# Six start offsets for the activations of the down products in a float32 decoder layer

## The chip, the cores and the metric

The kernel runs on one core of one Trainium2 chip. The metric is the device time of one execution in microseconds. The profile is of one execution of its own.

## The reference, cut to what matters

One decoder layer in float32, for 256 tokens of 2048 features. It has a feed-forward part at each end; between them stand a mixer (windowed attention beside a recurrent part) and a cross-attention, which the change does not touch. Each feed-forward part is

```
def swiglu(h, w_gate, w_up, w_down):
    return (jax.nn.silu(h @ w_gate) * (h @ w_up)) @ w_down

x = x + 0.5 * swiglu(rms_norm(x, ffn1_norm[l]), ffn1_w_gate[l], ffn1_w_up[l], ffn1_w_down[l])
```

with 5632 features inside (w_gate and w_up are 2048 x 5632, w_down is 5632 x 2048). The second feed-forward part is the same with its own weights, and a norm follows it.

## The kernel before

**Products.** All large products are made from pairs of float32r parts. A weight tile arrives as float32 (raw or raw2, by DMAs of SP's queue, `load`); ACT copies it into a float32r part `hi` (L299) and DVE subtracts to get the rest `lo` (L300), in `divide`. The activations are split in the same way into a hi and a lo part: xhi and xlo for the normed input, hhi and hlo for what goes into the down product. For each chunk of 128 features TensorE (PE) then runs three matmuls into the same bank of PSUM (`multiply`): activation hi by weight hi (L336), activation hi by weight lo (L337), activation lo by weight hi (L338). The activations are the stationary operand, 128 features by 128 tokens, loaded anew for each matmul; the weights are the moving one, as a rule 512 columns. `product` makes 512 output columns for all 256 tokens: it takes a unit of two chunks of weights at a time, and runs them for both halves of the tokens. So a unit is 12 matmuls.

**A feed-forward part.** `feed_forward` works in three groups (GROUPS) of four, four and three blocks of 512 inner features. For each block j it makes the gate product, applies silu on ACT (L415) into hb, makes the up product, and multiplies on DVE (L418). The block is then transposed in the background, by `transposed`: PE transposes 128 x 128 pieces of hb into PSUM (L347), two chunks at a time, ACT copies them to hhi (L352), and DVE subtracts to get hlo (L353). When the blocks of the group are through, four down products (n = 0 to 3) take all of the group's chunks, 16 or 12, out of hhi and hlo, and DVE adds half of the result to x (L427). So a group has 4 x 2 x 3 x 16 = 384 down matmuls, or 288 in the group of three blocks; the two feed-forward parts have 2112 in six groups.

**Tiles.** hhi and hlo are taken once per group, each from one buffer of the pool of its feed-forward part (bufs=1), as [128, 16, 256] float32r: 16 KB in each partition. A chunk is 256 tokens, 1024 bytes, and a matmul's stationary operand is half of it, 512 bytes. `Act.at` gives the slice. Each pool first takes a tile of 64 bytes (`aligned`) and so shifts all that follows. In the built program x, xhi, xlo, hhi, hlo, hb, raw, raw2, hi and lo, and the split activations of the mixer and the cross-attention, all start 480 bytes past a multiple of 512. In a weight tile of 288 columns, which is used once, the second half starts 1152 bytes after the first. Constants (the identity of the transposes among them) and the mixer's small tiles start elsewhere.

**Order.** Each engine runs its instructions in the order in which the Python code issues them. Background work (`Interleave`) is issued step by step between matmuls. Weight loads are issued some units ahead, and the hi and lo parts two units ahead.

Of the kernel before, what the change touches and what calls it, by code (L numbers as in the profile page):

```python
# [8 lines left out]
F32R = mybir.dt.float32r  # L9
# [6 lines left out]
P = 128  # L16
T = 256
# [103 lines left out]
def decoder_layer(ctx: ExitStack, tc: tile.TileContext, a: dict, out: bass.AP):  # L121
# [190 lines left out]
    def product(x: Act, w, skew=False):  # L312

        pw, _, nk, _, n = plan[at["product"]]
        assert pw.tensor is w.tensor
        at["product"] += 1
        o = [acc() for _ in range(2)]
        skewed = range(nk - AHEAD * KU - KU, nk, KU) if skew else range(nk, nk)
        for k in range(0, nk - KU * len(skewed), KU):
            bg.until(lambda: all(k + i in x.done for i in range(KU)))  # L320
            u = next_unit()
            for t in range(2):
                multiply(o[t][:, :n], x, u, k, t, nk)
                bg.tick()
        last = [(k, next_unit()) for k in skewed]
        for t in range(2):
            for k, u in last:
                multiply(o[t][:, :n], x, u, k, t, nk)
        return o
# [10 lines left out]
    def feat(tok, cols):  # L340


        b = tr()
        for i, col in enumerate(cols):
            for t in range(2):
                o = (2 * i + t) * P
                pe.transpose(b[:, o : o + P], tok[:, t, col : col + P], ident[:])  # L347
        return b[:].rearrange("p (c t) -> p c t", c=2)

    def split(x: Act, c, n, src):  # L350

        act.copy(x.at(0, c, n), src)  # L352
        dve.tensor_tensor(x.at(1, c, n), src, f32(x.at(0, c, n)), ALU.subtract)  # L353
        x.done |= set(range(c, c + n))
# [41 lines left out]
        return [r[:, t : t + 1] for t in range(n)]  # L396


    def feed_forward(sp, x, norm: Norm, wg, wu, wd, done, last=False):
        for gi, (j0, nj) in enumerate(GROUPS):  # L400
            h = Act(
                [sp.tile([P, 16, T], F32R, tag="hhi", name="hhi")],
                [sp.tile([P, 16, T], F32R, tag="hlo", name="hlo")], 16,
            )

            def transposed(hb, c):
                for q in range(2):
                    split(h, c + 2 * q, 2, feat(hb, [2 * q * P, (2 * q + 1) * P]))
                    yield

            for j in range(j0, j0 + nj):
                pg = product(norm.x, wg)
                hb = sp.tile([P, 2, 512], F32, tag="hb", name="hb", bufs=3)
                for t in range(2):
                    act.activation(hb[:, t, :], pg[t][:], AF.Silu, scale=norm.r[t])  # L415
                pu = product(norm.x, wu)
                for t in range(2):
                    dve.scalar_tensor_tensor(  # L418
                        hb[:, t, :], pu[t][:], norm.r[t], hb[:, t, :], ALU.mult, ALU.mult
                    )  # L420
                bg.spawn("feat", transposed(hb, 4 * (j - j0)))
            for n in range(4):
                end = gi == len(GROUPS) - 1
                pd = product(h, wd, skew=last and end and n == 3)
                for t in range(2):
                    xs = x[:, t, n * 512 : (n + 1) * 512]
                    dve.scalar_tensor_tensor(xs, pd[t][:], 0.5, xs, ALU.mult, ALU.add)  # L427
                if end:
                    done(n)
# [17 lines left out]
    with tc.tile_pool(name="f1", bufs=1, reuse_waits="tile") as sp:  # L447
        aligned(sp)
        at["pool"] = sp
        x = sp.tile([P, 2, D], F32, name="x")  # L450

        def col(n):
            return x[:, :, n * 512 : (n + 1) * 512]

        n1 = Norm(g_ffn1)
        for c in (slice(0, 256), slice(256, 512)):
            nc.sync.dma_start(x[:, :, c], W["x"][:, c].rearrange("(t p) n -> p t n", p=P))
            load(c.start // 256)
        for n in range(1, 4):
            nc.sync.dma_start(col(n), blk(W["x"], n))  # L460
            load(n + 1)
        for n in range(4):
            bg.spawn("feat", n1.block(n, col(n)))
        bg.spawn("const", late_vectors())
        hold = {}

        def done1(n):
            if n == 0:
                hold["n"] = Norm(g_mix)
            pool.dma_start(blk(x1d, n), col(n))  # L470
            bg.spawn("feat", hold["n"].block(n, col(n)))

        feed_forward(sp, x, n1, W["ffn1_w_gate"], W["ffn1_w_up"], W["ffn1_w_down"], done1)
        n2 = hold["n"]
        bg.drain()
        at["pool"] = None
# [666 lines left out]
    with tc.tile_pool(name="f2", bufs=1, reuse_waits="tile") as sp:  # L1143
# [18 lines left out]
        def done2(n):  # L1162
            for t in range(2):
                xs = x[:, t, n * 512 : (n + 1) * 512]
                act.activation(junk_t[:], xs, AF.Square, accum_out=ss[:, t, n : n + 1])  # L1165
                if n < 3:
                    pool.tensor_tensor(xs, xs, fin[:, n * 512 : (n + 1) * 512], ALU.mult)  # L1167

        feed_forward(
            sp, x, n4, W["ffn2_w_gate"], W["ffn2_w_up"], W["ffn2_w_down"], done2, last=True  # L1170
        )
# [42 lines left out]
```

## Time and profile before

| what | value |
|---|---|
| device time, median of 3 runs | 2328.53 us (2326.44 to 2334.17) |
| the profiled execution | 2327.99 us |
| its span, first to last instruction | 2326.3 us |
| mean granted TensorE clock | 0.998 |
| PE matmul records with xhi or xlo, 512 or 288 columns | 6048 |
| PE matmul records with hhi or hlo, 512 columns | 2112 |
| DVE L300, one of 128 x 1024 | 1226 ns mean, x769 |
| ACT L299, one of 128 x 1024 | 1048 ns mean, x769 |
| DMA, mean over the span | 186 GB/s |

How to read it. The page gives for each engine its busy time and its share of the span. PE counts matmul records, PEld the weight loads beside them. Matmuls overlap, and a record is longer than the distance to the next one; the distance is read from the starts in a timeline. Section 4 of the page follows the chain of work that ended last back to the start. In a group's line the last number is the idle time of its engine just before it, with what ended it. A windows view gives, for each stretch, its length, each engine's busy time with the number of instructions, the granted clock, and the share and rate of DMA.

The stretches of the six down groups in the span are 192.2 to 280.0 us, 457.2 to 544.9 and 677.6 to 746.5 in the first feed-forward part, and 1765.7 to 1853.4, 2030.6 to 2118.4 and 2251.1 to 2317.4 in the second.

### The profile page before, as it was taken

The page shows a single profiled execution, that of the slowest core. Times are in us where ns is not written, and L with a number is a line of the kernel's source. Part 1 is how long each engine was busy: PE and PEld are TensorE (multiplying, and loading weights), DVE is VectorE, ACT ScalarE, POOL GpSimd, SP SyncE. Part 2 cuts the span into 40 slices and gives each one's busy share as a digit, 9 for nine tenths or more (in the row PEclk, how much of TensorE's full clock was granted, in tenths as well). Part 3 has the DMA queues.
Part 4 walks back from the last instruction along what each step waited for, and adds up shares of the span by engine and source line. Part 5 has one row for each costly group of instructions (what it writes and reads, how often), then busy time and mean ns, then how long its engine had stood idle before and what let it go on. Part 6 is the DMA issues. An engine that isn't in the chain of part 4 may idle for free.

```text
span 2326.3 us, 27347 instructions
## 1 busy us (share of the span) xinstructions
PE 2303.9 (99%) x10853; PEld 1895.5 (81%) x10853; DVE 1259.5 (54%) x1395; ACT 1078.2 (46%) x1425; POOL 130.3 (6%) x192
## 2 busy tenths in 40 slices
PE   8999999999999999999999999999999999999998
PEld 7888888888888877888888878888888888888887
DVE  4545544554556477795444556555545544554545
ACT  5444344434445477444344446455444344434444
POOL 1000000000000000201220030001000000000001
PEclk9999999999999999999999999999999999999999
DMA  8555655556554544676432576648555555555553
GB/s 291 181 196 184 198 186 194 184 196 194 186 189 152 173 129 145 197 230 206 123 103 88 174 246 217 199 156 297 195 184 194 189 196 184 196 185 195 193 187 127
DMA packets 219856, 432.71 MB, mean 186 GB/s; under 512 B 14267, under 2 KB 17040, under 8 KB 219728
## 3 DMA queue, kind: packets, MB, share of 16 engines
q1 hardware_dynamic: 211520, 405.58, 53.3%
q0 software_dynamic: 8176, 25.38, 3.4%
q8 instruction: 85, 1.39, 0.2%
q14 instruction: 43, 0.35, 0.0%
q10 hardware_dynamic: 32, 0.01, 0.0%
HBM read 417.56 MB, written 13.11 MB: 185 GB/s over the span
## 4 chain that ended last, share of the span: by engine, by line
PE 93%; issue 4%; DVE 1%; DMA 1%; ACT 1%; POOL 1%; SPq 0%; POOLq 0%; ACTq 0%
PE acc L336 28%; PE acc L338 28%; PE acc L337 28%; PE tr L347 2%; PE mm L924 1%; PE tr L893 1%; POOL ml L1046 0%; PE mm L542 0%; DMA raw<-in_ffn_w_gate_dram 0%; PE tr L911 0%; ACT hi L299 0%; PE tr L994 0%; PE tr L907 0%; PE tr L581 0%; PE tr L589 0%
## 5 line engine op out<-in xcount | busy, mean ns | idle before, releaser
L300 DVE TENSOR_TENSOR lo<-raw,hi 128x1024 fp32r<-128x1024 f32 (+1 forms) x769 | 942.1, 1226 | 956.3 <-ACT hi L299 955.6
L299 ACT CAST hi<-raw 128x1024 fp32r<-128x1024 f32 (+1 forms) x769 | 805.5, 1048 | 1066.1 <-PE acc L338 1028.8
L336 PE MATMUL acc<-hi,xhi 128*128 128x512 f32 (+1 forms) x2016 | 798.7, 396 | 0.4 <-ACT xhi L373 0.4
L337 PE MATMUL acc<-lo,xhi 128*128 128x512 f32 (+1 forms) x2016 | 785.4, 390 | 0.0
L338 PE MATMUL acc<-hi,xlo 128*128 128x512 f32 (+1 forms) x2016 | 784.6, 389 | 0.0
L336 PEld LDWEIGHTS acc<-hi,xhi 128*128 128x128 f32 x2016 | 379.7, 188 | 80.3 <-issue 3.4
L338 PEld LDWEIGHTS acc<-hi,xlo 128*128 128x128 f32 x2016 | 379.1, 188 | 79.5 <-issue 1.0
L337 PEld LDWEIGHTS acc<-lo,xhi 128*128 128x128 f32 x2016 | 379.9, 188 | 78.0 <-issue 3.6
L336 PE MATMUL acc<-hi,hhi 128*128 128x512 f32 x704 | 275.5, 391 | 0.0
L338 PE MATMUL acc<-hi,hlo 128*128 128x512 f32 x704 | 274.2, 389 | 0.0
L337 PE MATMUL acc<-lo,hhi 128*128 128x512 f32 x704 | 274.0, 389 | 0.0
L338 PEld LDWEIGHTS acc<-hi,hlo 128*128 128x128 f32 x704 | 132.1, 188 | 27.5
L337 PEld LDWEIGHTS acc<-lo,hhi 128*128 128x128 f32 x704 | 132.2, 188 | 27.2
L336 PEld LDWEIGHTS acc<-hi,hhi 128*128 128x128 f32 x704 | 132.2, 188 | 26.8
L336 PE MATMUL acc<-hi,mthi 128*128 128x512 f32 x128 | 51.2, 400 | 0.0
L338 PE MATMUL acc<-hi,mtlo 128*128 128x512 f32 x128 | 50.1, 392 | 0.0
L337 PE MATMUL acc<-lo,mthi 128*128 128x512 f32 x128 | 49.9, 390 | 0.0
L1167 POOL TENSOR_TENSOR x<-x,fin 128x512 f32<-128x512 f32 x6 | 8.9, 1505 | 695.4 <-ACT junk L1165 695.4
L470 POOL DMA_DIRECT2D x1d<-x x4 | 3.0, 744 | 710.4 <-DVE x L427 710.4
L415 ACT ACTIVATE hb<-acc,rs 128x512 f32<-128x512 f32 x44 | 30.2, 690 | 19.5 <-PE acc L338 19.5
L352 ACT CAST hhi<-tr 128x512 fp32r<-128x512 f32 x44 | 25.7, 583 | 16.3 <-PE tr L347 16.3
L373 ACT ACTIVATE xhi<-tr,gains 128x256 fp32r<-128x256 f32 x48 | 22.0, 470 | 21.8 <-DVE xlo L374 16.1
(289 smaller groups left out, 1632.7 us busy)
## 6 DMA issues: line engine op xcount, KB each, us to landing
raw<-in_ffn_w_up_dram SPq DMA_DIRECT2D x88, 1024.0 KB, 5.1
raw<-in_ffn_w_down_dram SPq DMA_DIRECT2D x88, 1024.0 KB, 5.0
raw<-in_ffn_w_gate_dram SPq DMA_DIRECT2D x86, 1024.0 KB, 5.1
raw<-in_w_in_dram SPq DMA_DIRECT2D x136, 512.0 KB, 3.5
raw<-in_w_out_dram SPq DMA_DIRECT2D x32, 512.0 KB, 4.6
raw<-in_w_proj_attn_dram SPq DMA_DIRECT2D x16, 512.0 KB, 3.8
raw<-in_w_proj_rwkv_dram SPq DMA_DIRECT2D x16, 512.0 KB, 5.5
raw<-in_w_cross_kv_dram SPq DMA_DIRECT2D x16, 512.0 KB, 3.6
```

The source lines that it names most:

```text
L299: act.copy(hi[:, s], raw[:, s])
L300: dve.tensor_tensor(lo[:, s], raw[:, s], f32(hi[:, s]), ALU.subtract)
L336: pe.matmul(o, xh, hi[:, i, :], start=k + i == 0, stop=False)
L337: pe.matmul(o, xh, lo[:, i, :], start=False, stop=False)
L338: pe.matmul(o, xl, hi[:, i, :], start=False, stop=k + i == nk - 1)
L347: pe.transpose(b[:, o : o + P], tok[:, t, col : col + P], ident[:])
L352: act.copy(x.at(0, c, n), src)
L373: last = act.activation(self.x.at(0, c), b[:, j, :], AF.Copy, scale=g)
L415: act.activation(hb[:, t, :], pg[t][:], AF.Silu, scale=norm.r[t])
L893: pe.matmul(b[e][:, m * P : (m + 1) * P], x1[r, j, cs_], x2[r, j, cs_], start=True, stop=True,)
L924: pe.matmul(vb[:, o : o + P][:, r], lhs(e), rhs[:, r], start=first and e == 0, stop=True, **ek,)
L1167: pool.tensor_tensor(xs, xs, fin[:, n * 512 : (n + 1) * 512], ALU.mult)
```

## The change

Each of the six groups takes hhi and hlo out of a longer tile, of 16 x 256 + 64 elements (256 bytes more), and starts in it at another element: 8 times 1, 2, 4, 5, 6 and 7, that is 32, 64, 128, 160, 192 and 224 bytes. Both parts of a group have the same offset in their tile. The list is used up in the order of the groups, three in the first feed-forward part and three in the second.

```diff
+    places = [1, 2, 4, 5, 6, 7]
+
     def feed_forward(sp, x, norm: Norm, wg, wu, wd, done, last=False):
         for gi, (j0, nj) in enumerate(GROUPS):
-            h = Act(
-                [sp.tile([P, 16, T], F32R, tag="hhi", name="hhi")],
-                [sp.tile([P, 16, T], F32R, tag="hlo", name="hlo")], 16,
-            )
+            o = 8 * places.pop(0)
+
+            def part(name):
+                p = sp.tile([P, 16 * T + 64], F32R, tag=name, name=name)
+                return p[:, o : o + 16 * T].rearrange("p (c t) -> p c t", c=16)
+
+            h = Act([part("hhi")], [part("hlo")], 16)
```

Since the hhi tile is 256 bytes longer, the hlo tile begins 256 bytes later than before, and what lies behind both (hb, and raw2 in the second part) 512 bytes later.

## The prediction

> **What bounds the kernel now.** I read the page first: the busy times, the chain that ended last, then the groups of the down products.
>
> ```profile
> span 2326.3 us, 27347 instructions
> PE 2303.9 (99%) x10853; PEld 1895.5 (81%) x10853; DVE 1259.5 (54%) x1395; ACT 1078.2 (46%) x1425; POOL 130.3 (6%) x192
> ...
> PE 93%; issue 4%; DVE 1%; DMA 1%; ACT 1%; POOL 1%; SPq 0%; POOLq 0%; ACTq 0%
> ...
> L336 PE MATMUL acc<-hi,hhi 128*128 128x512 f32 x704 | 275.5, 391 | 0.0
> L338 PE MATMUL acc<-hi,hlo 128*128 128x512 f32 x704 | 274.2, 389 | 0.0
> L337 PE MATMUL acc<-lo,hhi 128*128 128x512 f32 x704 | 274.0, 389 | 0.0
> ```
>
> PE is busy for 99% of the span and carries 93% of the chain. The down products are 3 x 704 = 2112 matmuls, and nothing made them wait (idle 0.0). So PE's stream is the bound, and what counts in it is the distance from one matmul's start to the next, the pitch. The 389 ns of a record is no pitch: records overlap. The timeline of PE, early in the first down group, gives the pitch:
>
> ```profile
> 195.62 0.60 PE L347 MATMUL tr<-ident,hb 128*128 128x128 f32 x4
> 195.98 0.48 PE L336 MATMUL acc<-hi,hhi 128*128 128x512 f32 x1
> 196.30 0.40 PE L337 MATMUL acc<-lo,hhi 128*128 128x512 f32 x1
> 196.53 0.40 PE L338 MATMUL acc<-hi,hlo 128*128 128x512 f32 x1
> ...
> 197.92 0.39 PE L338 MATMUL acc<-hi,hlo 128*128 128x512 f32 x1
> ...
> 200.19 0.39 PE L336 MATMUL acc<-hi,hhi 128*128 128x512 f32 x1
> ...
> 202.91 0.39 PE L336 MATMUL acc<-hi,hhi 128*128 128x512 f32 x1
> ```
>
> The first column is the start. From 196.30 to 197.92 there are 7 steps: 1.62 / 7 = 231 ns. From 200.19 to 202.91 there are 12: 2.72 / 12 = 226.7 ns. So after the transposes the stream runs unsettled for some nine matmuls and then settles at 226.7 ns. The starts in the trace show the same after every interruption (229, 233, 236, 224, 231, 236, 228, 233, 231 ns, then 226 or 227 up to the next transposes), for xhi and for hhi alike. The settled starts of the whole trace lie on one grid of 6.67 ns.
>
> What a column costs is read where the clock was halved (timeline of PE at 820 to 830 us; the windows view gives a granted clock of 0.50 for 822.2 to 825.6):
>
> ```profile
> 824.35 0.44 PE L338 MATMUL acc<-hi,xlo 128*128 128x288 f32 x1
> 824.59 0.44 PE L336 MATMUL acc<-hi,xhi 128*128 128x288 f32 x1
> 824.83 0.44 PE L337 MATMUL acc<-lo,xhi 128*128 128x288 f32 x1
> ...
> 826.11 0.29 PE L338 MATMUL acc<-hi,xlo 128*128 128x288 f32 x1
> ...
> 828.91 0.29 PE L338 MATMUL acc<-hi,xlo 128*128 128x288 f32 x1
> ```
>
> At half clock 288 columns take 240 ns, 0.833 ns each, so 0.417 ns at full clock: 288 columns are 120.0 ns, 512 are 213.3 ns. Later, at full clock, 21 steps take 2.80 us: 133.3 ns each. So every settled matmul pays **13.3 ns over its columns**, at 288 as at 512 columns (226.7 - 213.3), or 32 column times, two steps of that grid. At half clock it pays nothing. The float32 transposes pay nearly nothing too: four take 0.60 us with a last record of 272 ns (their group's mean), so (600 - 272) / 3 = 109 ns, against 2 x 128 x 0.417 = 106.7 ns if each column passes twice. I read this as follows (argued, not shown): the surcharge comes from the stream and the weight load of the next matmul both reading SBUF, and it is paid only where the stream takes a new column every clock. If so, it may depend on the two addresses, and the change moves one of them.
>
> The Trainium skill (TensorE: Matmul & The Clock Gate, Part 2, step on LDWEIGHTS) states that the array has two independent SBUF read ports and that loading the next weights takes no read bandwidth from the running matmul. By that rule the start address of the weights costs nothing and the sum is zero. The trace does not bear it out as far as I read the 13.3 ns; no row here separates the load from the other causes that they could have.
>
> **The change part by part.**
>
> *Instructions, waits, DMAs.* None is added or removed: 15,868 instructions before and after, in the same order. 2112 matmuls read their stationary operand elsewhere, 44 ACT copies (L352, 583 ns) and 44 DVE subtractions (L353, 688 ns) write it there. One wait grows: SP's first load of gate weights for the second feed-forward part waits for one more semaphore of POOL's DMAs. Queued behind it are all later weight loads, and the ACT copies (L299) wait for those. But it asks for a count of 64, where the neighbouring semaphores are asked for 160 and 176, so that transfer is from much earlier in the mixer. Cost: 0.
>
> *The ACT and DVE writes.* Before, no row has the same copy at another start, so I bound it. If each took twice as long, a copy would add 0.6 us and a subtraction 0.7 us, some seven times a group. In the window of the first group (192.2 to 280.0 us) ACT is busy 34.83 of 87.8 us and DVE 45.22, so the cover is over 40 us. Without that cover it would be 44 x 1.27 = 56 us. A gain is also worth nothing here. I take 0.
>
> *Pools.* The padding moves hlo by 256 bytes, and hb, with raw2 in the second part, by 512. DMAs and casts keep their start within 512 bytes; 0.
>
> *The 2112 matmuls.* Before, every float32r operand of PE starts 480 bytes past a multiple of 512, stationary and moving (from the built program's allocation). Afterwards hhi starts at 0, 32 and 96 in the first part and 128, 160 and 192 in the second, hlo 256 further, and the moving weights stay at 480. There are 384 matmuls in groups of 16 chunks and 288 in those of 12. The six windows of the down groups add up to 486.2 us, of which 2112 x 0.2267 = 478.7 us are pitch. Each ns of mean pitch is worth 2.1 us.
>
> Bounds for that ns: from below, the surcharge falls from 13.3 to the 2.3 ns of the transposes: -11.0 x 2112 = -23 us. From above, each matmul runs at the longest unsettled pitch, 236 ns: +9.3 x 2112 = +20 us. Three rows lie between these, and they are nearest:
> - Moving operand elsewhere: in the 288-column tile the second half starts 1152 bytes after the first, so it lies 128 bytes off the common phase. The 21 steps from 826.11 to 828.91 go through both halves in turn, and none of their starts departs from an even 133 ns by more than the 10 ns of the view; the trace's own starts have 131 to 134 ns in the settled steps of both.
> - Stationary operand elsewhere: the float32 matmuls have it at 32, 128, 224, 288 and 480 past a multiple of 512. Their pitch at 128 columns is 111 to 112 ns both at 480 and at 32. These pay little surcharge, so they weigh less.
> - Other parts in the same place (xhi, mthi, yahi, hhi) all settle at 226.7 ns.
>
> The value I take is a change of **0 ns**: the only float32r row with unequal phases shows none. Sum: 2327.99 us (the profiled execution: a span of 2326.3 and 1.7 around it) + 0 = 2328.0. The median of the runs shown lies 0.5 above that, so I forecast **2328.5 us**.
>
> **The rivals.**
>
> *B: the stream no longer settles (slower).* The settled pitch is a state in which load and stream, starting at one phase, fall in step with the grid. Set apart, they may keep running as they do after an interruption. Price: 231.3 - 226.7 = 4.6 ns, x 2112 = +9.8 us, 2338 us. If they settle one grid step later instead, +6.67 x 2112 = +14.1 us, 2342.6 us. In half of the groups alone: +5 to +7. It decides from a mean pitch of 230.0 ns in the six groups (3.3 ns more). For it: the unsettled runs exist, with the same instructions and addresses, so the pitch does hang on phases. Against it: the 128-byte row settles.
>
> *C: the surcharge shrinks (faster).* If equal phases make load and stream collide, other starts free them. One grid step less is -6.67 x 2112 = -14.1 us, 2314.4 us; down to the transposes' 2.3 ns it is 2305 us. For it: 13.3 ns that half clock does not pay. Against it: 128 bytes apart did not help. The load is hidden either way, since its record (187 to 192 ns) ends before the next matmul's start, so a shorter load alone would bring nothing.
> The Trainium skill (TensorE: Matmul & The Clock Gate, Back-to-back issue gap) gives an isolated matmul's gap as N / 2.4 + 2.5 ns, 215.8 for 512 columns. By it this rival would end at -10.9 x 2112 = -23 us; the trace does not agree, with its settled 226.7.
>
> *D: the change does not do what it says.* The built program has the new addresses in all 2112 matmuls, so I leave it out.
>
> **How the numbers follow.** A measurement of this kernel can tell about 0.3% from no change, 7.0 us, or 3.3 ns of mean pitch. No dependence, or one in so few groups or of both signs that it stays below that: 0.42. B beyond it: 0.37, more than C because the settled pitch is lower than the unsettled mean, so that there is more to lose by leaving that state than one row shows to gain. C beyond it: 0.21. The likeliest case's own range is 2323 to 2334. The range reaches to one grid step in all groups on either side, 2314.4 and 2342.6, with 1.5 us for runs: 2313 to 2344. Outside lie a surcharge all but gone and a pitch near the longest seen, 0.2 together.
>
> **What would show it.** In the changed profile, the starts inside each down group: 226.7 ns in all six is my case; 231 or 233 in some is B, 220 or less is C, and the groups that differ name the starts that matter. The groups L336 to L338 with xhi must keep their means, and DVE, ACT and the waits as well. I am wrong if a group's window of 87.8 us moves by over 1.3 us, or if a new wait stands ahead of L299 or L336.

## The result, and the profile after

The changed kernel takes 2341.64 us (median of 3 runs, 2341.32 to 2342.9) against 2328.53: 13.1 us more, a ratio of 1.0054 with a 95% interval of 1.0041 to 1.0067. The forecast was no change. The time lies inside the stated range, 1 us below the price of rival B's second form (one grid step more in every down matmul, 2342.6 us). That it lies so close is partly luck: the down groups grew by 11.5 us, as the windows below show, and not by that form's 14.1.

The page of the profile after, in the order in which the page of before was read:

```profile
span 2341.2 us, 27347 instructions
PE 2316.6 (99%) x10853; PEld 1895.9 (81%) x10853; DVE 1258.6 (54%) x1395; ACT 1078.1 (46%) x1425; POOL 131.1 (6%) x192
...
PE 93%; issue 4%; DVE 1%; POOL 1%; ACT 1%; DMA 1%; SPq 0%; POOLq 0%; ACTq 0%
...
L336 PE MATMUL acc<-hi,xhi 128*128 128x512 f32 (+1 forms) x2016 | 798.8, 396 | 1.2 <-ACT xhi L373 1.2
...
L336 PE MATMUL acc<-hi,hhi 128*128 128x512 f32 x704 | 278.7, 396 | 0.0
L337 PE MATMUL acc<-lo,hhi 128*128 128x512 f32 x704 | 278.3, 395 | 0.0
L338 PE MATMUL acc<-hi,hlo 128*128 128x512 f32 x704 | 277.6, 394 | 0.0
```

The same instructions, the same chain of 93% PE, and still no idle time before the down products: nothing waits that did not wait before. DVE, ACT and POOL have kept their sums within 1 us. Only the matmul records of hhi and hlo have grown, from 389 to 391 ns to 394 to 396.

The windows view shows where the time came from. It has one line for each of the six down groups, cut at the first and the last start of their matmuls: the window, its length, PE's busy time (records of PE), the granted clock, DMA's share, GB/s. Before:

```profile
192.40:280.20 87.80, 87.80 (x392) 72.67 (x392) 45.22 (x43) 34.83 (x34) 0.00 (x0) 1.00 0.59 192
```

(this line has PEld, DVE, ACT and POOL too). After:

```profile
192.40:282.60 90.20, 90.20 (x393) 1.00 0.59 187
459.80:550.00 90.20, 90.20 (x392) 1.00 0.57 187
682.80:753.10 70.30, 70.30 (x320) 1.00 0.44 149
1775.60:1865.90 90.30, 90.30 (x393) 1.00 0.56 187
2043.10:2131.70 88.60, 88.60 (x393) 1.00 0.57 190
2264.40:2332.20 67.80, 67.80 (x296) 1.00 0.35 125
sum 497.40, PE 497.40; mean PE 82.90
```

Each group is longer, by 0.8 us (192 bytes, the fifth) to 2.6 us, and the six together by 497.4 - 485.9 = 11.5 us. The spans differ by 2341.2 - 2326.3 = 14.9 us. Nearly all of what is left lies between the third group and the fourth, in the mixer and what follows it: 753.1 to 1775.6, 1022.5 us, instead of 746.7 to 1765.9, 1019.2 us. In this stretch the profile after has two pieces of 3.4 us at about half the granted clock (0.50 for 864.9 to 868.3 us, 0.51 for 895.6 to 899.1), the profile before only one (822.2 to 825.6). At half clock a piece can lose at most half its length, 1.7 us (an estimate). In runs below whose instructions in it are the same, the stretch takes from 1019.9 us (fine_and_far, one such piece) to 1023.0 (pad_only, three), so I do not count it to the change.

The timeline of PE after, in the first group (32 bytes) and in the fifth (192 bytes); the first column is the start:

```profile
229.62 0.40 PE L336 MATMUL acc<-hi,hhi 128*128 128x512 f32 x1
...
232.43 0.40 PE L336 MATMUL acc<-hi,hhi 128*128 128x512 f32 x1
```

```profile
2079.70 0.39 PE L336 MATMUL acc<-hi,hhi 128*128 128x512 f32 x1
...
2082.45 0.39 PE L336 MATMUL acc<-hi,hhi 128*128 128x512 f32 x1
```

Twelve steps lie between the two starts of each: 2.81 / 12 = 234 ns and 2.75 / 12 = 229 ns, where before had 226.7. The trace's own starts, from the 15th step after an interruption on, give the settled pitch of each group:

| offset of hhi and hlo | settled pitch | pattern of the steps, ns |
|---|---|---|
| 0 (before) | 226.67 | 226, 227, 227 |
| 32 | 233.33 | 232, 234, 233, 234, 233, 234 |
| 64 | 233.33 | 236, 231, 236, 230 |
| 128 | 232.4, then 233.3 | 228, 230, 232, 241, 232, 231, 232 in the first of four long stretches; 229 and 237 or 238 in turn in the others |
| 160 | 233.33 | 232, 238, 230 |
| 192 | 228.88 | 226, 229, 232 |
| 224 | 233.33 | 233, 235, 230, 235, 234, 234, 231, 235 |

So the stream does settle, into a pattern that repeats and spans whole steps of the 6.67-ns grid: 34 steps for a matmul at 0, 35 at most of the others, 103 for three matmuls at 192. At 128 bytes it settles into two different patterns, though the operands of all four stretches lie the same. The products with xhi keep 226.67.

### The profile page after: what moved, and what is told of

It is laid out like the page before. It is cut to its first block, busy times and chain, and to the rows that moved or that the text cites. A ratio compares the mean times of both kernels' runs of the same rounds, so it can differ in the third digit from the quotient of the medians.

```text
span 2341.2 us, 27347 instructions
## 1 busy us (share of the span) xinstructions
PE 2316.6 (99%) x10853; PEld 1895.9 (81%) x10853; DVE 1258.6 (54%) x1395; ACT 1078.1 (46%) x1425; POOL 131.1 (6%) x192
## 4 chain that ended last, share of the span: by engine, by line
PE 93%; issue 4%; DVE 1%; POOL 1%; ACT 1%; DMA 1%; SPq 0%; POOLq 0%; ACTq 0%
PE acc L336 28%; PE acc L337 28%; PE acc L338 28%; PE tr L347 2%; PE mm L930 1%; PE tr L899 1%; POOL ml L1052 1%; DMA raw<-in_ffn_w_gate_dram 0%; PE mm L548 0%; ACT hi L299 0%; PE tr L917 0%; PE tr L1000 0%; PE tr L913 0%; PE tr L587 0%; PE tr L595 0%
## 5 line engine op out<-in xcount | busy, mean ns | idle before, releaser
L299 ACT CAST hi<-raw 128x1024 fp32r<-128x1024 f32 (+1 forms) x769 | 804.9, 1047 | 1077.8 <-PE acc L338 1040.4
L336 PE MATMUL acc<-hi,xhi 128*128 128x512 f32 (+1 forms) x2016 | 798.8, 396 | 1.2 <-ACT xhi L373 1.2
L336 PEld LDWEIGHTS acc<-hi,xhi 128*128 128x128 f32 x2016 | 379.6, 188 | 81.4 <-issue 3.6
L336 PE MATMUL acc<-hi,hhi 128*128 128x512 f32 x704 | 278.7, 396 | 0.0
L336 PEld LDWEIGHTS acc<-hi,hhi 128*128 128x128 f32 x704 | 132.2, 188 | 31.2
L336 PE MATMUL acc<-hi,mthi 128*128 128x512 f32 x128 | 51.2, 400 | 0.0
```

Of the source, the lines that this page charges most:

```text
L299: act.copy(hi[:, s], raw[:, s])
L336: pe.matmul(o, xh, hi[:, i, :], start=k + i == 0, stop=False)
```

## The experiments

The expectations name three theories. **R**: what counts is how far the start of the stationary operand lies from that of the moving one. **S**: the stationary operand's own start counts. **H**: the cost comes from how hlo lies to hhi, not from either one's distance to the weights. Each run is compared with the kernel before on the same chip. The diffs of pad_only, fine_and_far, weights_follow, sixteen, plain_float32 and half_load are against the changed kernel, the others against the kernel before; "..." marks lines left out. Where there is no interval, it is a single execution. Windows lines have the columns named above, either with PE alone or with PEld, DVE, ACT and POOL as well.

**pad_only: the longer tiles, no offset.**

```diff
-    places = [1, 2, 4, 5, 6, 7]
+    places = [0, 0, 0, 0, 0, 0]
```

> The longer tiles stay, all six groups start at their first element. What differs from the kernel before is only that hlo lies 256 bytes further from hhi, and hb and raw2 512 further. Theory R (the distance between the start of the activations and the start of the weights, within 256 bytes, sets the pitch at which the stream settles): 226.7 ns in all six groups, 2328 us. Rival H (the distance between hhi and hlo, which the padding changed by 256 bytes, is what costs): 229 to 233 ns in the groups as after the change, 2335 to 2342 us.

Measured: 2329.68 us against 2328.31, ratio 1.0003 (0.9993 to 1.0012). Windows of its first two groups:

```profile
193.00:280.80 87.80, 87.80 (x393) 72.68 (x392) 45.23 (x43) 34.83 (x34) 0.00 (x0) 1.00 0.59 192
458.00:545.70 87.70, 87.70 (x392) 72.64 (x391) 45.13 (x43) 34.83 (x34) 0.00 (x0) 1.00 0.59 192
```

Both have before's length, and all six groups settle at 226.67. H falls: hlo lies to hhi here exactly as after the change, and that costs nothing. Nor does the padding, with hb 512 bytes further. The cost is in the offsets.

**fine_and_far: which offsets cost.** Offsets of 4, 8, 16, 96, 256 and 512 bytes.

```diff
-    places = [1, 2, 4, 5, 6, 7]
+    places = [1, 2, 4, 24, 64, 128]
-            o = 8 * places.pop(0)
+            o = places.pop(0)
-                p = sp.tile([P, 16 * T + 64], F32R, tag=name, name=name)
+                p = sp.tile([P, 16 * T + 128], F32R, tag=name, name=name)
```

> Offsets of 4, 8, 16, 96, 256 and 512 bytes in the six groups, in tiles that are 512 bytes longer, so that both parts have the same start within 512. Theory R with a period of 256 bytes: 226.7 ns at 256 and 512, more at 96, about 233; if what counts is a unit of 16 or 32 bytes, 4 and 8 stay at 226.7. Rival S (each operand's own start counts, not the distance): 226.7 at 512 alone. By R the whole is about 2334 to 2340 us.

Measured: 2335.04 us against 2328.31. Its six groups:

```profile
192.40:282.30 89.90, 89.90 (x392) 1.00 0.58 187
459.50:548.80 89.30, 89.30 (x393) 1.00 0.59 189
681.50:750.20 68.70, 68.70 (x321) 1.00 0.45 152
1770.10:1860.70 90.60, 90.60 (x393) 1.00 0.56 186
2037.90:2125.60 87.70, 87.70 (x392) 1.00 0.57 192
2258.30:2324.30 66.00, 66.00 (x296) 1.00 0.38 128
```

The last two, at 256 and 512 bytes, are as long as before's fifth and sixth (87.8 and 66.0). Settled pitches in order: 232.39, 230.66, 226.67, 234.29, 226.67, 226.67. So the offset counts modulo 256 bytes, as far as these two multiples show. There is no free unit below which it does not matter, since a single element (4 bytes) costs 5.7 ns; 16 bytes cost nothing here.

**hi_or_lo: one part at a time.** hhi and hlo get offsets of their own: (32, 0), (0, 32), (128, 0), (0, 128), (192, 0), (0, 192) bytes.

```diff
+    places = [(8, 0), (0, 8), (32, 0), (0, 32), (48, 0), (0, 48)]
...
+            oh, ol = places.pop(0)
...
+            h = Act([part("hhi", oh)], [part("hlo", ol)], 16)
```

> One part is offset at a time: hhi by 32, hlo by 32, hhi by 128, hlo by 128, hhi by 192, hlo by 192 bytes, in the order of the groups. hhi is loaded for two matmuls of three, hlo for one. Theory R, each load paying for itself: with hhi alone two thirds of the rise of both (231 ns at 32 and 128), with hlo alone one third (229 ns). If instead the settled state is one of the whole stream, a single odd load takes the stream out of step and both cost the full step, 233.3 ns. Rival H: the same for hhi alone and hlo alone at one offset, and unlike the run with both.

Measured: 2338.93 us against 2328.31; settled pitches 231.83, 233.35, 233.33, 231.10, 228.89, 231.05. Its first two groups:

```profile
192.50:282.20 89.70, 89.70 (x393) 1.00 0.59 188
459.40:549.60 90.20, 90.20 (x392) 1.00 0.58 187
```

Were the cost paid by each load that lies apart, hlo alone, one load in three, would cost a third: 226.67 + 6.67 / 3 = 228.9 ns. At 32 bytes it costs the whole step (second line, as long as with both). At 192 bytes hlo alone costs 4.4 ns, twice what both together cost. So this is not a sum over loads. The other expectation, the full step for either part, holds for hlo at 32 and hhi at 128 bytes only: hhi at 32 costs 5.2 ns, hlo at 128 4.4. The pitch seems to belong to the rhythm in which the stream as a whole settles; which rhythm that will be, none of the theories says.

**all_moved: another common place.** In the kernel before, a constant of 32 bytes more moves the operands of all the large products to a multiple of 512.

```diff
+    cpool.tile([P, 8], F32, name="nudge")
```

> The kernel before with a tile of 32 bytes more among the constants, so that activations, weights and all other tiles behind it start 32 bytes further (at multiples of 512 instead of 480 past). Theory R: distances are the same, 226.7 ns everywhere and 2328 us. Rival S (a load that starts at 480 past a multiple of 512 is the cheap one, at 0 it costs 233.3 as in the first group after the change): all 9120 wide matmuls pay 6.7 ns more, 2389 us.

Measured: 2327.93 us against 2328.31, ratio 1.0 (0.9991 to 1.0009), 226.67 ns throughout. S falls: at the same distance the operands' own place did not count.

**weights_follow: the change, and the weights with it.** The hi and lo parts of the down products' weights get the same six offsets as the activations.

```diff
...
+    moved = {i: 8 * [1, 2, 4, 5, 6, 7][j // 4] for j, i in enumerate(downs)}
...
-        hi = wp.tile([P, KU, n], F32R, tag="hi", name="hi")
-        lo = wp.tile([P, KU, n], F32R, tag="lo", name="lo")
+        o = place(of[u])
+
+        def part(name):
+            p = wp.tile([P, KU * n + 64], F32R, tag=name, name=name)
+            return p[:, o : o + KU * n].rearrange("p (a n) -> p a n", a=KU)
+
+        hi, lo = part("hi"), part("lo")
```

> The change stays, with its six offsets for the activations; the weight parts hi and lo of the down products are given the same six offsets in longer tiles, so that the two operands of each matmul start at the same place within 256 bytes again. Theory R (only the distance counts): all six groups settle at 226.7 ns, 2328 us. Rival S (the start of the activations alone counts): as after the change, 233 ns and 2342 us. The gate and up products keep the old places: 226.7 ns.

Measured: 2328.67 us against 2329.43, ratio 0.9998 (0.9989 to 1.0008). The first, second and fourth group:

```profile
192.50:280.30 87.80, 87.80 (x393) 1.00 0.60 192
457.50:545.30 87.80, 87.80 (x393) 1.00 0.59 192
1767.60:1855.40 87.80, 87.80 (x393) 1.00 0.59 192
```

The activations lie where the change put them, and yet the 90.2 us are 87.8 again; all six groups settle at 226.67. This is the run that decides for R: what the change cost is the distance between the two operands, and moving the other one by as much takes the cost away.

**scan_weights: 64 distances.** Activations as before, and the weight parts of each feed-forward product at another of 64 offsets, 0 to 252 bytes.

```diff
+    def place(i):
+        last = len(plan) - 34
+        return i if i < 34 else i - last + 30 if i >= last else 0
...
+        o = place(of[u])
...
```

> The activations stay as in the kernel before; the weight parts of each product of the feed-forward parts start at another offset, 0, 4, 8 and so on to 252 bytes (64 places; the 34 products of the first part take 0 to 132, those of the second 120 to 252). Theory R: weights 32, 64, 96, 128, 160, 192, 224 bytes further are activations 224, 192, 160, 128, 96, 64, 32 bytes further, so 233.3, 228.9, 233.3, 233.1, 234.3, 233.3, 233.3 ns, and 226.7 at 0. Open is whether any place settles lower, on 220.0 ns, one step of 6.67 under the kernel before; as no place so far does (seven multiples of 32, and 4, 8, 16), I expect none. With most places at 230 to 234 ns, 66 products of 96 or 72 matmuls pay some 6 ns: +35 us, about 2363 us.

Measured: 2370.14 us against 2329.43; 226.67 ns at 0 and at 112 bytes, 227.8 at 28, 60 and 108, and 228.9 to 240.0 everywhere else (240.0 is 36 grid steps, at 20, 116, 132 and 196). Four offsets occur in both parts; at 132 the two products settle apart, at 235.7 and 240.0. No distance is below 226.67. At the multiples of 32, weights moved by d cost what activations moved by 256 - d did: 64 gives 228.88 (activations 192: 228.88), 160 gives 234.29 (activations 96: 234.29), 128 gives 233.3 (activations 128: 232.4 and 233.3), and 32, 96, 192 and 224 give 233.3. Below 32 bytes the mirror fails: weights at 252, 248 and 240 give 228.9, 232.2 and 233.33, activations at 4, 8 and 16 gave 232.39, 230.66 and 226.67.

**sixteen: all activations 16 bytes off.** Of the activation offsets, 16 bytes came nearest to 0. Here xhi, xlo, hhi and hlo all have it.

```diff
+            def part(name):
+                p = xtp.tile([P, KD * T + 64], F32R, tag=name, name=name)
+                return p[:, 4 : 4 + KD * T].rearrange("p (c t) -> p c t", c=KD)
+
+            self.x = x or Act([part("xhi")], [part("xlo")], KD)
...
+    places = [4] * 6
...
+            o = places.pop(0)
```

> xhi, xlo, hhi and hlo all start 16 bytes further than in the kernel before, in tiles 256 bytes longer; the weights and the activations of the mixer and the cross-attention stay. In the run with offsets of 4 to 512 bytes the group at 16 settled at 226.7 ns too, and sooner after each interruption: its 288 matmuls with eight interruptions took 68.68 us, against 68.88 at equal starts. If that holds for the gate and up products and the mixer's input products, some 150 interruptions save about 25 to 35 ns each, 4 to 5 us: 2323 to 2325 us. If the stream settles elsewhere with another history, products at 230 ns or more would make it slower by 10 us and more.

Measured: 2331.0 us against 2327.41, ratio 1.001 (1.0001 to 1.0019): a little slower. The down groups keep 87.7 us. The first gate and up products show where it is lost: windows of 20 to 190 us, of before and then of this kernel, have 771 and 769 records of PE in the same 170 us.

```profile
20.00:190.00 170.00, 170.00 (x771) 1.00 0.62 208
```

```profile
20.00:190.00 170.00, 170.00 (x769) 1.00 0.64 207
```

The starts show why: of the 36 uninterrupted stretches of more than 40 matmuls with xhi or xlo, 30 settle at 226.67, and six, at the same distance, in patterns of 231 to 235 with a mean of 233.3. The six have 617 matmuls; at 6.67 ns that is 4.1 us, where the medians differ by 3.6. At 16 bytes there are two settled rhythms, and which one a product falls into differs. The weights at 240 bytes had the second one's mean, so there the mirror may fail only because the stream fell into the other rhythm.

**plain_float32: the change, with the down products read as float32.**

```diff
+            h, l = hi[:, i, :], lo[:, i, :]
+            if getattr(x, "plain", False):
+                xh, xl, h, l = f32(xh), f32(xl), f32(h), f32(l)
...
+            h.plain = True
```

> The change with its six offsets, but the down products read both operands as plain float32 instead of float32r, so that a column passes at half the rate (512 columns take 428 to 429 ns in the mixer's float32 products). If the six places cost because load and stream compete at one column per clock, the six groups now have the same pitch within 1 ns, about 429, and the whole takes about 2328 + 2112 x 0.202 = 2755 us. If the places cost at any rate, the groups differ by 2 to 7 ns as after the change.

Measured: 3664.49 us against 2327.41. The size was off: a float32 matmul becomes two records of 429 ns, not one. PE's timeline:

```profile
300.40 1.02 PE L341 MATMUL acc<-hi,hlo 128*128 128x512 f32 x2
301.26 1.02 PE L339 MATMUL acc<-hi,hhi 128*128 128x512 f32 x2
302.12 1.02 PE L340 MATMUL acc<-lo,hhi 128*128 128x512 f32 x2
```

Each line is one matmul's two records, 0.86 us after the last. The trace's starts give 429.17 to 429.20 ns per record in all six groups, whatever the offset. If the columns pass twice in each record, that is 2 x 213.3 = 426.7 and 2.5 ns. So at these six distances float32 pays nothing, and float32 rows could not have shown the cost. That this is because its columns pass at half the rate is not shown: a load of 188 ns also has twice the time beside such a record. The Trainium skill (TensorE: Matmul & The Clock Gate, Back-to-back issue gap) gives 2.5 ns over the columns for an isolated matmul; taken so, the float32 records agree with it, and the float32r matmuls do not (13.3 at best).

**half_load: the surcharge against the loaded bytes.** Offsets 0, 0, 0, 32, 128, 192. The kernel leaves out half of most down products.

```diff
+            q = slice(0, 64 if hasattr(x, "half") and 0 < k + i < nk - 1 else P)
+            pe.matmul(o[q], xh[:, q], hi[:, i, :], start=k + i == 0, stop=False)
...
+            h.half = True
```

> In the down products only the first 64 tokens of each half are loaded and multiplied for all chunks but the first and the last: half of those products is left out. Columns of the weights are unchanged, 512. The six groups start at 0, 0, 0, 32, 128 and 192 bytes. If the 13.3 ns over the columns are paid for the bytes that the next load reads, a load of half the bytes pays half, and the groups at 0 settle at 220.0 ns, one step of the grid lower (the whole about 2328 - 14 = 2314 to 2325 us by what the other places then cost). If they are paid once per matmul whatever is loaded, they stay at 226.7 ns.

Measured: 2338.35 us against 2327.41. Windows of the first two groups, both at offset 0:

```profile
192.70:281.70 89.00, 89.00 (x392) 54.74 (x391) 45.25 (x43) 34.62 (x34) 0.00 (x0) 1.00 0.58 189
458.90:547.90 89.00, 89.00 (x392) 54.75 (x391) 45.25 (x43) 34.63 (x34) 0.00 (x0) 1.00 0.58 189
```

The third number is PEld: with half of the bytes the loads take 54.7 us instead of 72.7 (134 ns each instead of 188), but the group has become longer, 89.0 us instead of 87.8. The settled pitch rises to 230.1 ns at 0, and is 231.79, 229.81 and 228.40 at 32, 128 and 192. Both expectations missed. The 13.3 ns are not simply paid by the loaded byte: with half of the bytes the stream fell into a longer rhythm. Whether it is the load's length that does this stays open, since these matmuls also make results for 64 tokens instead of 128.

**no_shift_tile: the same distance by another way.** The kernel before without the tile of 64 bytes at the head of each pool (`aligned`): then the operands of the pools keep their own starts.

```diff
-        sp.tile([P, 16], F32, name="shift")
+        pass
```

> The kernel before without the 64-byte tile at the head of the three pools: hhi and hlo, and the activations of the mixer's and the cross-attention's products (1056 matmuls), start 64 bytes before the weights' place, which is 192 bytes past it within 256; xhi and xlo stay at equal starts. Theory R: these 3168 matmuls behave as the fifth group after the change (192 bytes) did, 228.9 ns, in all six down groups: +2.2 x 3168 = +7.0 us, 2335 us. Rival (only the change's own tiles matter): 226.7 ns and 2328 us.

Measured: 2334.84 us against 2329.15, ratio 1.0026 (1.0016 to 1.0035). Its first two groups:

```profile
192.20:280.80 88.60, 88.60 (x392) 1.00 0.58 190
458.00:546.60 88.60, 88.60 (x392) 1.00 0.59 190
```

The length is that of the changed kernel's group at 192 bytes, and so are the pitch, 228.88, and the pattern, 226, 229, 232; the mixer's and the cross-attention's products have it too. R had forecast both numbers.

**halves_apart: the row that the forecast leaned on.** In the 288-column tile the rows become 320 elements, so that both halves lie at the common place, and in the down products' weight tiles 544, so that each second half lies 128 bytes off.

```diff
...
+        row = 320 if n == 288 else 544 if units[u][0].shape[0] == DFF else n
+
+        def part(name):
+            return wp.tile([P, KU, row], F32R, tag=name, name=name)[:, :, :n]
```

> Two edits to the kernel before. In the 288-column tile each half gets a row of 320 columns, 1280 bytes, so that both halves start at the activations' place within 256 bytes; in the tiles of the down products the second half starts 128 bytes further than the first, as it did in the 288-column tile, by rows of 544 columns. If the forecast's reading was right that halves 128 bytes apart pay nothing more, the 288-column product keeps 133.3 ns and the six down groups 226.7 ns. If that row misled, because the raised state was already in it or because its few matmuls were read too coarsely, the 288-column product falls below 133.3 ns, or the down groups rise to between 228 and 233 ns, about +5 to +14 us.

Measured: 2338.0 us against 2329.15. First group, and PE's timeline in the 288-column product:

```profile
192.20:282.10 89.90, 89.90 (x393) 1.00 0.57 187
```

```profile
829.03 0.29 PE L342 MATMUL acc<-hi,xlo 128*128 128x288 f32 x1
...
831.93 0.29 PE L340 MATMUL acc<-hi,xhi 128*128 128x288 f32 x1
```

Between the two lie 22 steps: 2.90 / 22 = 131.8 ns. The trace's starts give 131.6 to 131.7, where before has 133.0 to 133.3. With both halves at equal starts the 288-column matmul takes 1.6 ns less than it did before, and the down products with every second half 128 bytes off settle at 232.2 ns, 5.5 more. So the row did hold the cost.

## Why the prediction was wrong

- **What bounds the kernel**: right. PE's stream; what the change cost appeared in the pitch.
- **Instructions, waits, ACT and DVE writes, pools at 0**: right. The sums of ACT and DVE moved by less than 1 us, no wait appeared ahead of L299 or L336, and pad_only moved the time by 0.03% with an interval around none.
- **"Each ns of mean pitch is worth 2.1 us"**: right. The groups grew by 11.5 us, 5.4 ns over 2112 matmuls, and the time by 13.1: nothing hid the longer pitch.
- **"The value I take is a change of 0 ns: the only float32r row with unequal phases shows none"**: this step failed. The row of the 288-column tile mixes starts that are equal with starts 128 bytes off, and had nothing beside it with equal starts alone. I took its 133.3 ns, 13.3 over the columns as at 512, for the undisturbed state; halves_apart shows that state at 131.7. The cost was in the row, 1.6 ns on the mean of both halves, in a view that rounds to 10 ns and in starts of 131 to 134 ns that I called settled. At equal starts the surcharge is 13.3 ns at 512 columns and 131.7 - 120.0 = 11.7 at 288, so its being 13.3 at both confirmed nothing. (The 120.0 assumes, as the prediction did, that a matmul at half clock takes its columns' time and no more. No run tests that.)
- **The other two rows** could not show it either. Float32 matmuls of 512 columns paid nothing at the six distances (plain_float32), so the float32 rows were no measure of float32r, which the text had allowed for. "Other parts in the same place" all had equal starts, and say nothing on unequal ones.
- **Rival B**: the right direction, and nearly the right price. The 5.4 ns are more than the 3.3 that it asked for. It said that load and stream "fall in step with the grid" when they start at one phase. That the settled pitch hangs on relative starts is what weights_follow shows. The stream does not stay unsettled; it settles one grid step later in five groups (in the one at 128 bytes a little less, 6.4 ns on the mean) and a third of a step later in the sixth. Priced by settled pitch this is 384 x (6.66 + 6.66 + 6.67 + 2.21) + 288 x (6.4 + 6.66) = 12.3 us; 11.5 were measured. Part of the difference is in the matmuls right after an interruption, which took some 229 ns before and 233 after in five of the groups, so they lost less than a settled one.
- **Rival C**: refuted. None of 64 distances was below 226.67 ns. "128 bytes apart did not help" was right, but from the misread row; it costs 6.4 ns.
- **The surcharge as load and stream sharing SBUF** was called argued, and remains so. For it: moving the stationary operand alone changes the pitch. Against its simplest form: with half of the loaded bytes the pitch was longer (half_load). The Trainium skill's rule that loading the next weights takes no read bandwidth from the running matmul (TensorE: Matmul & The Clock Gate, Part 2, step on LDWEIGHTS) would have the start of the stationary operand cost nothing. The runs do not agree with that: moving the activations alone cost up to 7.6 ns a matmul (96 bytes, 234.29). Whether the two reads are the reason, no run shows.

Open is what the 13.3 ns at equal starts are, why the period is 256 bytes, why the mirror between weights and activations fails below 32 bytes, and what decides between two rhythms at one distance. No version tried beats the kernel before.

## What to carry to other kernels

Where PE runs float32r matmuls back to back, look in the built program for the start of the stationary and of the moving operand, and bring them to the same place modulo 256 bytes: one small tile at the head of each pool decided it here, and it was worth 0.26% (no_shift_tile); against the changed kernel's six places equal starts were worth 0.54%. Read the pitch from the starts of many matmuls, not from the length of records. A row shows that a thing costs nothing only if a row without that thing stands beside it.

## What the runs showed of the hardware

- The settled pitch of a 512-column float32r matmul took values from 226.67 to 240.0 ns when only the distance between its operands' starts was changed; 256 and 512 bytes were as good as 0. The repeating patterns that were followed span whole steps of 6.67 ns.
- It is no sum over the loads: one load in three apart can cost as much as all three (hlo alone at 32 bytes, 233.35 ns). At some distances the stream was found in two states: 226.67 and 233.3 ns at 16 bytes, 232.4 and 233.3 at 128, 235.7 and 240.0 with the weights at 132.
- Matmuls with half the stationary operand, whose loads took 134 ns instead of 188, had a longer pitch, not a shorter one: 230.1 instead of 226.67 ns.
- Plain float32 took 429.2 ns per record of 512 columns, two records for each matmul, at all six distances.
